# A K/V place inside a shared table tile against a tile of its own, in a hybrid attention and state-space step

## The chip, the core and the metric

The kernel runs on one core of a Trainium2 chip, alone. The metric is the device time of one execution in microseconds. Five engines work side by side, each through its own instruction queue: PE (matmul), DVE, ACT, POOL, and SP, which issues transfers. They meet at semaphores.

## The reference

One layer of a decoder trunk is computed for a prompt of 512 tokens and for one new token of each of 8 sequences. Per token: RMSNorm with modulation, one input projection, then two parallel parts (8 heads of forgetting attention and a diagonal state-space model, S5), one output projection, a gated residual and a final norm.

```python
h = _rmsnorm(x, g_norm) * (1 + scale[:, None]) + shift[:, None]
p = h @ w_in                                    # q, k, v, z_att, fl, u, z_ssm
# prompt: causal attention over 512 tokens; S5 scan over 512 steps
# decode: each of 8 sequences attends to 4096 past rows in 32 pages
k_past = cache_k[l][page_table].reshape(nb_s, -1, ATT_HEADS, HEAD_DIM)
v_past = cache_v[l][page_table].reshape(nb_s, -1, ATT_HEADS, HEAD_DIM)
s_past = einsum('nthd,nphd->nhtp', q, k_past) * scale + suffix + cnew
pr = softmax(concatenate([s_past, s_new]))
o = einsum('nhtp,nphd->nthd', pr, v_past) + pr_new * v_new
...
mix = concatenate([att * silu(z_att), ssm], axis=-1)
return x + gate[:, None] * (mix @ w_out)
```

All of it is float32. The past rows of K and V are 2 x 64 MB, most of what is read.

## The kernel before

**Two streams of work.** `prompt()` makes the prompt's part: the projections, the S5 phase (`ssm_phase`), attention (`attn`), the output projection. `decode()` works through 64 units of K and 64 of V, each a [128 x 2048] tile of 1 MB (8 sequences x 8 chunks of 512 rows). A K unit is one indirect gather issued by POOL (`gather`); POOL multiplies two of its four parts by q and DVE the other two, ACT sums one part and DVE reduces three into the scores `sc`. A V unit is four pages of 256 KB, each issued by SP (`page`: a load of the page number from `prow`, then the transfer); page j fills the partitions j, j+4, j+8 and so on. PE alone reads V units, into the accumulator `pv`. V of a unit follows K ten units behind (`LAG`).

**Where units lie.** `kvt()` hands out five places in turn: units 0 and 1 of every five go into the arena `arA`, the other three into the ring `kva` (tiles named kv). `arA` is one SBUF tile of 128 x 12864 float32 in which an `Arena` cuts out column ranges by hand: first two K/V places of 2048 columns, then m8, m9, pz0, pz1 and others. The later columns hold what S5 works on (X, U, Hst, gr, gi, ta) and pz, the decode weights that PE reads beside V; the columns of the two places hold small tables for S5 (vec, an, cn, bn0, bn1, lam, mag, ...) before the first K unit comes.

**What sets the order.** Nothing runs where it is written. `Plan.add` records each operation with the exact cells that it touches, `Plan.order` plays the recorded work through a table of costs and picks at each step the ready operation with the lowest key (its number, plus `RANK` by part and engine, plus `TURN` by step), and `issue` hands all of it to the engines in that order. The layer below then adds the semaphore waits. It goes by the tiles of the program: where it cannot tell two accesses of one tile apart, it orders them as the plan has them, with a wait. All operations are recorded through one helper, so the profile shows nearly all of them at one line, L560; L770 and L771 are `page`.

In `ssm_phase`, four rounds q work through gr, gi, ta, tb_ on DVE; each ends with four steps that write 64 partitions of Hst:

```python
V.tensor_mul(ta, gr, (wr, wi)[i])
V.tensor_mul(tb_, gi, (wi, wr)[i])
for gh in range(2):
    rows = slice(64 * gh, 64 * gh + 64)
    V.tensor_tensor(Hst[64 * i:64 * i + 64, g0:g0 + 4, 1:], ta[rows], tb_[rows], ...)
```

In the trace these are the DVE steps TENSOR_TENSOR arA<-arA 64x256. The names in the trace: arA and arB are the arenas, kv the ring, mm, tr, q and pv are PSUM tiles, w and qk hold weights, hT the normed prompt, sc scores.

Of the kernel before, what the change touches and what calls it, by code (L numbers as in the profile page):

```python
# [26 lines left out]
NG = 32  # L27
# [7 lines left out]
AK = 50.25  # L35
# [7 lines left out]
    "e": [-9378, -12179, -17159, -20880, -7129, -3740],  # L43
    "k": [104, -5305, 5846, 4790, -7019, -5420],
    "v": [3806, 19560, 20236, 14005, 5324, 4733],
    "a": [8219, -3833, 15753, 8603, -6405, -12004],
    "b": [4421, -21319, -12840, -4994, 6926, 7303],
    "c": [18435, -15510, 7896, -467, -6963, 4257],
    "d": [-1470, -22153, -9218, 15147, -17350, 1823],
# [6 lines left out]
    ],  # L56
    "d": [
        4795, 6712, 1132, 822, -677, -645, 961, 271, -1496170991788475374953747049762376384512,
        -1591416928304185771207288444586741267955712, -15098942732813808483527931238350312571928576,
        -24799897758268515043116245559766386923798528, -24799957837215446326703523194706079082610688,  # L60
        -22512543007516039504454457036779652038787072, -25002668463705283549291374098367526039715840,
        -29873932956061450741600537962173382751420416, -40522577413528868136961928381290713911918592,
        -656491679919118699897556014178701078953984, -642743040628110155344957322818619348877312,
        -62820075513418327778175664689033788658810880, -31965431385341246944872999212492328399798272,
        -32190172543624901591007866841660712573468672, -662031355379155916244683619416854488940544,
        -106016004103496999941151100604199043334144, -662031355379155916244683619416854488940544,
        -661537939003796413634398241935909585944576, -661537939003796413634398241935909585944576,
        -662031355379155916244683619416854488940544, 29, 268848616566157757319417064656553902080,
        -57870939370597673452547150700062179328, -334202152619078557839858215189636710400,
        -222824342116560032991352920573877420032, -525646652941556557807465459025453252608, 423,  # L70
        -3114873590464629931083284636405596160, -383115191651056941544106031232183173120,
        -386230065241521609254121178825750478848, -355144111998878565346486905165379010560,
        -64470733409659124669137878287273426944, -536450766638600210376872646191683207168,
        -442246846342626279238667934105147015168, -550661652511238445432594584645721391104,
        -647779345490100210706929550522845233152, -647779345490100210706929550522845233152,
        -586050504110921321804771991115117101056, -444201669966760682229681522505072771072,
        -377431746165918168997425053696, -372824414621113103280408363008, -372824414621113103280408363008,
        -1504693897653695397102722742222848, -1504693897653695397102722742222848,
        -1935208998083464046905965777610648584192, -9878709610588491638058856337331527352320,
        -21914172760187454673687602720408004984832, -19930248552996642265506833922142981062656,  # L80
        -35472622895141998128347479877853969907712, -17942108367032813781047609379774116397056,
        -21914172760187454673687602720408004984832, -22295873388539040105921799003631698051072,
        13483862984301235780786450122486151380992, 35430370893032923703480572196236596084736,
        -62262870277911108193245080439253630976, -31852081206274918821088721330146711175168,
        -57312208504676145128161655563302161350656, 296716, 799, 1375, 1151, -6151969445025, -890395425558722,
        -156758765851781088, -156758765851781088, -196442193167641696, 6151969415511, -18965520271643, -37818,
        -893, -1054, 20313999, 20314729, 21951, -11686584, -11698753, -9559, -1020863, -496961, 487489, 540935,
        53762, -671, 105, -169, 28310960870464548, -895, -191, -463, 238, 2053, 5138895284143988736,
        5138895284143988736, 1074408661396193280, 2120, 337884334897070912, 337884334897070336,
        337884334897069824, -32645103648539280408576, 838, 833, 863, 2307, -25873837905436944899419790114816,  # L90
        -25873837905436944899419790114816, -25873837905436944899419790114816,
        -52309082650344698289716512553959424, -167332142037711083914639474098700288,
        -182522220296334633003524770624438272, -115023059387366376401550924689965056,
        -167306268199805658525976698141278208, -115023059387366376401550924689965056,
        -313445072502919342502520957467361280, -345069178162099110757908700360343552,
        -1586434662390481495591677170024448, -4400390153836027197102747969126400,
        -6000515168275917989466142700208128, 7115305423999194397066622140416, 0,
        7115305423999201152466063196160, 6755399441065209
    ],
# [69 lines left out]
class Arena:  # L169


    def __init__(self, t, start=0):
        self.t, self.at, self.names = t, start, {}

    def tile(self, shape, dtype, name, bufs=1, room=0):
        n = max(room, int(np.prod(shape[1:])))
        if name not in self.names:
            self.names[name] = [self.at, n, bufs, 0]
            self.at += n * bufs
            assert self.at <= self.t.shape[1], (name, self.at)  # L180
        e = self.names[name]
        assert n <= e[1], name
        o = e[0] + e[1] * (e[3] % e[2])
        v = self.t[:shape[0], o:o + int(np.prod(shape[1:]))]
        e[3] += 1
        if len(shape) > 2:
            ax = "abcd"[:len(shape) - 1]
            v = v.rearrange(f"p ({' '.join(ax)}) -> p {' '.join(ax)}", **dict(zip(ax, shape[1:])))
        return v


class Plan:
# [128 lines left out]
    def cost(self, eng, method, args, outs, ins, kw):  # L321
        n = max([r[4] for r in outs + ins], default=1)
        ps = any(r[5] for r in outs + ins)
        if "dma" in method:
            return (955 if "indirect" in method else 560) if eng == "Pool" else 800 if method == "dma_page" else 480
# [242 lines left out]
def tile_fox_s5_step(ctx, tc, x_prompt, x_sample, c_prompt, c_sample, cache_k, cache_v, cache_logf,  # L568
# [18 lines left out]
    plan.own(arA)  # L587
    plan.own(arB)
# [37 lines left out]
    for at, lst in (("kv", (("vec", 128), ("xs64", 128), ("bad", 128), ("an", 256), ("ldt", 32), ("cn", 512), ("bn0", 1024),  # L626
# [1256 lines left out]
```

## Time and profile before

| what | value |
|---|---|
| median of 3 runs | 615.48 us (613.07 to 615.69) |
| the profiled execution | 620.36 us, its span 618.0 us |
| TensorE clock granted, mean | 0.888 |
| busy PE / DVE / ACT / POOL | 478.5 / 388.5 / 286.9 / 264.5 us |
| moved by DMA | 178.71 MB, mean 289 GB/s |
| DMA queues' share of 16 engines | 50.5% (SP's), 29.1% (POOL's) |

The profiled execution is one run with the profiler on; sums are made against its span of 618.0 us, and it lies 0.8% above the median. Busy time is per engine and overlaps; which wait ends last in a stage tells what that stage costs.

### The profile page before, as it was taken

The page shows a single profiled execution, that of the slowest core. Times are in us where ns is not written, and L with a number is a line of the kernel's source. Part 1 is how long each engine was busy: PE and PEld are TensorE (multiplying, and loading weights), DVE is VectorE, ACT ScalarE, POOL GpSimd, SP SyncE. Part 2 cuts the span into 40 slices and gives each one's busy share as a digit, 9 for nine tenths or more (in the row PEclk, how much of TensorE's full clock was granted, in tenths as well). Part 3 has the DMA queues.
Part 4 walks back from the last instruction along what each step waited for, and adds up shares of the span by engine and source line. Part 5 has one row for each costly group of instructions (what it writes and reads, how often), then busy time and mean ns, then how long its engine had stood idle before and what let it go on. Part 6 is the DMA issues. An engine that isn't in the chain of part 4 may idle for free.

```text
span 618.0 us, 10616 instructions
## 1 busy us (share of the span) xinstructions
PE 478.5 (77%) x3203; PEld 252.1 (41%) x3203; DVE 388.5 (63%) x660; ACT 286.9 (46%) x1369; POOL 264.5 (43%) x201
## 2 busy tenths in 40 slices
PE   2768999779956573835676996979979798999872
PEld 2237347636522252614543442434434453433321
DVE  5999788494467927955764766565573744765321
ACT  2532366442244812424453698566675863432000
POOL 3188399551134843442444445263362344441000
PEclk9969999969986875975897997988999897999975
DMA  7993897664758986695899779899999699998850
GB/s 239 398 356 106 322 288 275 237 229 132 266 190 283 332 336 229 224 373 154 297 343 383 283 290 351 317 398 336 351 391 360 252 358 417 351 348 290 276 205 3
DMA packets 56849, 178.71 MB, mean 289 GB/s; under 512 B 18354, under 2 KB 33112, under 8 KB 39256
## 3 DMA queue, kind: packets, MB, share of 16 engines
q1 hardware_dynamic: 46560, 109.35, 50.5%
q0 software_dynamic: 10016, 68.63, 29.1%
q8 instruction: 25, 0.41, 0.3%
q14 instruction: 32, 0.26, 0.1%
q10 hardware_dynamic: 216, 0.06, 0.0%
HBM read 172.53 MB, written 5.47 MB: 288 GB/s over the span
## 4 chain that ended last, share of the span: by engine, by line
PE 38%; DMA 27%; DVE 12%; SPq 7%; ACT 6%; issue 5%; POOL 2%; POOLq 0%; DVEq 0%; ACTq 0%
PE mm L560 29%; DMA arA<-in_cache_v_dram 8%; DVE arA L560 7%; DMA kv<-in_cache_v_dram 6%; DMA arA<-in_cache_k_dram,kidx 5%; PE pv L560 5%; PE tr L560 4%; DMA kv<-in_cache_k_dram,kidx 4%; SPq L771 4%; SPq L770 2%; ACT arA L560 2%; DVE sc L560 2%; ACT arB L560 2%; DMA w<-in_w_out_dram 1%; DVE arB L560 1%
## 5 line engine op out<-in xcount | busy, mean ns | idle before, releaser
L560 POOL TENSOR_TENSOR kv<-kv,qs 128x1024 f32<-128x1024 f32 x38 | 89.6, 2359 | 79.6 <-DMA kv<-in_cache_k_dram,kidx 61.1
L560 ACT ACTIVATE kv<-kv 128x64 f32<-128x64 f32 x304 | 73.1, 243 | 78.6 <-DVE kv L560 66.7
L560 PE MATMUL mm<-hT,w 128*128 128x512 f32 x224 | 103.3, 617 | 0.0
L560 POOL DMA_INDIRECT kv<-in_cache_k_dram,kidx x38 | 37.9, 997 | 109.5 <-DVE sc L560 18.9
L560 DVE TENSOR_REDUCE sc<-kv 128x24 f32<-128x1536 f32 x38 | 66.3, 1747 | 17.0 <-POOL kv L560 16.8
L560 PE MATMUL mm<-w,hT 128*64 128x256 f32 (+1 forms) x384 | 62.7, 399 | 17.4 <-DVE arA L560 13.3
L560 POOL TENSOR_TENSOR arA<-arA,qs 128x1024 f32<-128x1024 f32 x26 | 61.4, 2364 | 30.9 <-DMA arA<-in_cache_k_dram,kidx 24.0
L560 ACT ACTIVATE arA<-arA 128x64 f32<-128x64 f32 (+2 forms) x219 | 52.8, 245 | 40.1 <-DVE arA L560 37.3
L560 PEld LDWEIGHTS mm<-w,hT 128*64 128x64 f32 (+1 forms) x384 | 53.1, 204 | 28.1 <-DVE arA L560 14.2
L560 PEld LDWEIGHTS mm<-hT,w 128*128 128x128 f32 x224 | 43.5, 199 | 51.2 <-issue 50.7
L560 DVE TENSOR_TENSOR kv<-kv,q 128x1024 f32<-128x1024 f32 x38 | 46.1, 1212 | 26.0 <-DMA kv<-in_cache_k_dram,kidx 25.5
L560 PE MATMUL pv<-kv,arA 128*32 128x512 f32 x304 | 45.5, 679 | 21.6 <-DMA kv<-in_cache_v_dram 21.5
L560 ACT ACTIVATION_READ_ACCUMULATOR kv<-kv 128x1 f32 x304 | 57.2, 188 | 0.0
L560 DVE TENSOR_REDUCE sc<-arA 128x24 f32<-128x1536 f32 x26 | 45.4, 1747 | 13.4 <-POOL arA L560 12.9
L560 DVE TENSOR_TENSOR arA<-arA 128x32 f32<-128x32 f32 (+8 forms) x80 | 31.9, 420 | 27.7 <-DMA arA<-in_cache_v_dram 25.5
L560 ACT ACTIVATION_READ_ACCUMULATOR arA<-arA 128x1 f32 x208 | 39.3, 189 | 0.0
L560 PE MATMUL pv<-arA 128*32 128x512 f32 x208 | 30.3, 663 | 11.0 <-DMA arA<-in_cache_v_dram 11.0
L560 POOL DMA_INDIRECT arA<-in_cache_k_dram,kidx x26 | 25.5, 981 | 23.7 <-PE pv L560 12.9
L560 DVE TENSOR_TENSOR arA<-arA,q 128x1024 f32<-128x1024 f32 x26 | 31.4, 1209 | 5.4 <-DMA arA<-in_cache_k_dram,kidx 5.3
L560 PE MATMUL mm<-w,arB 128*128 128x512 f32 x64 | 31.6, 650 | 2.9 <-DMA w<-in_w_out_dram 2.9
L560 ACT ACT_TABLE_LOAD x23 | 29.5, 1283 | 6.3 <-DVE sc L560 3.3
L560 ACT ACTIVATE arB<-tr 128x512 f32<-128x512 f32 (+3 forms) x46 | 20.8, 479 | 25.0 <-PE tr L560 15.3
(253 smaller groups left out, 765.9 us busy)
## 6 DMA issues: line engine op xcount, KB each, us to landing
kv<-in_cache_v_dram SPq DMA_DIRECT2D x152, 256.0 KB
arA<-in_cache_v_dram SPq DMA_DIRECT2D x104, 256.0 KB
w<-in_w_in_dram SPq DMA_DIRECT2D x11, 1024.0 KB
w<-in_w_ada_dram SPq DMA_DIRECT2D x9, 1024.0 KB
qk<-in_w_ada_dram SPq DMA_DIRECT2D x2, 1024.0 KB
kv<-in_x_prompt_dram SPq DMA_DIRECT2D x2, 1024.0 KB
w<-in_w_out_dram SPq DMA_DIRECT2D x2, 1024.0 KB
qk<-in_w_out_dram SPq DMA_DIRECT2D x2, 1024.0 KB
```

What stands on the lines that cost most here:

```text
L560: fn(*args, **kw)
L770: v = nc.values_load(at, engines=[mybir.EngineType.SP], skip_runtime_bounds_check_because="pages of the pool")
L771: return nc.sync.dma_start(out[0], in_[bass.DynSlice(v, 1)].rearrange("n r x -> (n r) x"))
```

## The change

Two tiles of their own, kv0 and kv1 (named kv_83 and kv_84 in the built program), take the places of the first 4096 columns of arA, which shrinks by as much. The early tables move with them: the small ones into kv0, bn0 and bn1 into kv1. `kvt()` hands out kv1 and kv0 in turn where it handed out the arena's two. The planner's cost of a page on SP goes from 800 to 970 ns. `RANK` and `TURN`, which hold the order, are new throughout. The same operations are recorded as before. The helper's line is now L593, `page` L809 and L810.

```diff
-AK = 50.25
+AK = 34.25
 RANK = {
-    "e": [-9378, -12179, -17159, -20880, -7129, -3740],
+    "e": [-14411, -25244, -19742, -16758, -20859, -859],
...
 class Arena:
     def __init__(self, t, start=0):
-        self.t, self.at, self.names = t, start, {}
+        self.t, self.at, self.names, self.sub = t, start, {}, {}
     def tile(self, shape, dtype, name, bufs=1, room=0):
+        if name in self.sub:
+            return self.sub[name].tile(shape, dtype, name, bufs)
...
-            return (955 if "indirect" in method else 560) if eng == "Pool" else 800 if method == "dma_page" else 480
+            return (955 if "indirect" in method else 560) if eng == "Pool" else 970 if method == "dma_page" else 480
...
-    plan.own(arA)
-    plan.own(arB)
+    places = [ar.tile([128, 2048], F32, name=f"kv{i}") for i in range(2)]
+    for t in (arA, arB, *places):
+        plan.own(t)
...
-    for name, size, bufs in (("kv", 2048, 2), ("m8", NG * (NCH + 1), 1), ("m9", 2304, 1), ("pz0", 1024, 1), ("pz1", 1024, 1),
+    for name, size, bufs in (("m8", NG * (NCH + 1), 1), ("m9", 2304, 1), ("pz0", 1024, 1), ("pz1", 1024, 1),
...
+    for t, lst in ((places[0], (("vec", 128), ("xs64", 128), ("bad", 128), ("an", 256), ("ldt", 32), ("cn", 512), ("tmpc", 128),
+                                ("th", 64), ("nn", 64), ("lam", 64), ("mag", 64), ("sn_t", 128), ("dt", 32), ("lrd", 32),
+                                ("am1", 32), ("t1", 32), ("t2", 32), ("den2", 32))),
+                   (places[1], (("bn0", 1024), ("bn1", 1024)))):
+        a = Arena(t)
+        for name, size in lst:
+            a.tile([128, size], F32, name=name)
+            tb.sub[name] = a
...
-        if kvp[1] is not None and n % 5 in (0, 1):
-            return kvp[1].tile([128, 2048], F32, name="kv", bufs=2)
+        if n % 5 in (0, 1):
+            kvp[1] += 1
+            return places[kvp[1] % 2]
         return kva.tile([128, 2048], F32, name="kv")
```

**SP in the S5 phase.** The four pages of one V unit in arA, before; in brackets are the semaphores each waits for. DMAHW and DMASW are landings of transfers issued by SP and by POOL; each transfer of SP waits for the eighth before it.

```order
L771 DMA arA<-in_cache_v_dram 32x2048 [waits DMASW5_49,DMAHW4_49,DVE_49,Activation_49]
L770 TENSOR_LOAD prow
L771 ISA
L771 DMA arA<-in_cache_v_dram 32x2048 [waits DMAHW5_49,DVE_49]
...
L771 DMA arA<-in_cache_v_dram 32x2048 [waits DMAHW6_49]
...
L771 DMA arA<-in_cache_v_dram 32x2048 [waits DMAHW7_49,DVE_49]
```

The same unit now:

```order
L810 DMA kv_84<-in_cache_v_dram 32x2048 [waits DMASW5_49,DMAHW3_49,DVE_49,Activation_49]
L809 TENSOR_LOAD prow
L810 ISA
L810 DMA kv_84<-in_cache_v_dram 32x2048 [waits DMAHW4_49]
...
L810 DMA kv_84<-in_cache_v_dram 32x2048 [waits DMAHW5_49]
...
L810 DMA kv_84<-in_cache_v_dram 32x2048 [waits DMAHW6_49]
```

The second and the fourth page no longer wait for DVE; the first still waits for the K unit that lay there.

**DVE at the same place,** the third round of S5 with its steps on Hst (64x4x64), before:

```order
L560 TENSOR_TENSOR arB<-mm,arB 64x32 [waits PE_49]
L560 TENSOR_TENSOR arB<-mm,arB 64x32
L560 TENSOR_TENSOR arA<-arA 64x4x64 [waits DMAHW5_49,DMAHW4_49,DMAHW6_49,DMAHW3_49,DVE_49]
L560 TENSOR_TENSOR arA<-arA 64x4x64 [waits DMAHW6_49,DMAHW5_49]
L560 TENSOR_TENSOR arB<-mm,arB 64x32 [waits PE_49]
```

And now:

```order
L593 TENSOR_TENSOR arB<-mm,arB 64x32 [waits PE_49]
L593 TENSOR_TENSOR arB<-mm,arB 64x32
L593 TENSOR_TENSOR arA<-arA 64x4x64 [waits DVE_49]
L593 TENSOR_TENSOR arA<-arA 64x4x64
L593 TENSOR_TENSOR arB<-mm,arB 64x32 [waits PE_49]
```

The steps stand where they stood; their waits for landings of V pages (DMAHW) are gone.

**PE at the end,** from the last scoring (the first product of each fence) on, before; pv rows are V units, mm rows with w or qk and arB are the output projection of the prompt:

```order
L560 MATMUL tr_476<-ident_95,mx_475 8x128
L560 MATMUL pv_346<-kv_474,arA_81 32x512 x4
L560 MATMUL pv_346<-kv_478,arA_81 32x512 x4
...
L560 MATMUL mm_537<-w_503,arB_82 128x512 x4
L560 MATMUL mm_537<-w_502,arB_82 128x512 x4
L560 MATMUL pv_346<-arA_81 32x512 x8
...
L560 MATMUL mm_539<-qk_505,arB_82 128x512 x4
L560 MATMUL mm_539<-qk_504,arB_82 128x512 x4
```

And now:

```order
L593 MATMUL tr_478<-ident_97,mx_477 8x128
L593 MATMUL pv_348<-kv_476,arA_81 32x512 x4
L593 MATMUL pv_348<-kv_480,arA_81 32x512 x4
...
L593 MATMUL mm_531<-qk_507,arB_82 128x512 x4
L593 MATMUL mm_531<-qk_506,arB_82 128x512 x4
...
L593 MATMUL mm_541<-qk_507,arB_82 128x512 x4
L593 MATMUL mm_541<-qk_506,arB_82 128x512 x4
...
L593 MATMUL mm_539<-w_505,arB_82 128x512 x4
L593 MATMUL mm_539<-w_504,arB_82 128x512 x4
```

One more projection group now stands between the last scoring and the last V unit. On SP two of the stores of y now stand directly ahead of the last unit's four pages, where before one stood ahead of an earlier unit.

More of the change, by code (lines that the diff above doesn't have):

```diff
@@ L42 @@
 RANK = {
-    "e": [-9378, -12179, -17159, -20880, -7129, -3740],
[L44 to L49, printed above, removed]
+    "e": [-14411, -25244, -19742, -16758, -20859, -859],
+    "k": [18397, -15550, 8591, 7953, -12240, -6546],
+    "v": [-9085, 12810, 29056, -6364, 8398, -88],
+    "a": [11830, 1247, 22656, -16707, -7001, -6671],
+    "b": [-4277, -15538, -32314, 5089, -4287, 4755],
+    "c": [22088, -2732, 13492, -3209, -10103, 18389],
+    "d": [-8859, -26750, 3767, 21817, 7887, 437],
 }
@@ L52 @@
     "e": [
[3 rows of a table removed]
[3 rows of a table added]
     ],
     "d": [
[L58 to L96, printed above, removed]
@@ L97 @@
-        -6000515168275917989466142700208128, 7115305423999194397066622140416, 0,
-        7115305423999201152466063196160, 6755399441065209
[66 rows of a table added]
     ],
     "p": [
[10 rows of a table removed]
+        -109, 15, 45, -222, 8065, 9977, 1242, 643, 11365, -490, -52652, -6798, -44945, -48680, -1887, 28198,
+        28540, 29652, 29644, 0, -81618134797231127511251775270519595367956360312478778144486273843200, 0,
+        -18373, 0, -5779, 0, 21, 0, 42497621235554144873424195564477612032,
+        42497621235554144873424195564477612032, 42497621235554144873424195564477612032, -565, -7857, 1978, 9191,
@@ new lines @@
+        2407, 29285, 29684, -15877, -1343, -14927, -13852, 10816, 4340329273, 4340489340, 4340480743, -2764,
+        6198, -877, 245, 35416023233, 4473, -422, 7706, 10730, 12618, 144, 11243, 1224, 34937, 8517930800,
+        8517932124, 8517931362, 8517932246, 26435093416, 42435016302974063345664, 42435016302974063345664,
+        42435016302974063345664, 127839947401898655481856, 35353015588, 84869968819851064508416,
+        -1690998123043453585927812582427070562304, 5353620633031020109512982426285980516352,
@@ new lines @@
+        3662912131573146954534552254631685128192, 7044618756074473695440795008713051078656,
+        7044618756074473695440795008713051078656, 7582, 30998918359293790244597937974071315286540810434117632,
+        30998918350070824823780670117331434463764334923218944,
+        30998918441720504955920491051401361979759328965427200, 77417908100936604894132400352864162356920320,
+        -16905104742501867612434523550789078857285632, 8509675778110755114046603593808924454694118303146704896,
+        7786776666398760674500781184652224857538262789739511808,
@@ L111 @@
+        12460596675090748511242188559371858885320015025069359104
     ],
@@ L622, in tile_fox_s5_step @@
     late = Arena(arA)
-    for name, size, bufs in (("kv", 2048, 2), ("m8", NG * (NCH + 1), 1), ("m9", 2304, 1), ("pz0", 1024, 1), ("pz1", 1024, 1),
+    for name, size, bufs in (("m8", NG * (NCH + 1), 1), ("m9", 2304, 1), ("pz0", 1024, 1), ("pz1", 1024, 1),
                              ("y_sv", 512, 1), ("u_s", 512, 1), ("oT", 32, 1)):
         late.tile([128, size], F32, name=name, bufs=bufs)
-    for at, lst in (("kv", (("vec", 128), ("xs64", 128), ("bad", 128), ("an", 256), ("ldt", 32), ("cn", 512), ("bn0", 1024),
[3 rows of a table removed]
+    for t, lst in ((places[0], (("vec", 128), ("xs64", 128), ("bad", 128), ("an", 256), ("ldt", 32), ("cn", 512), ("tmpc", 128),
[6 more added lines that the diff above has]
+            tb.sub[name] = a
+    for at, lst in (("m8", (("cT", 1024), ("tC", 512), ("tB", 512))),
                     ("m9", (("Bsw", 512), ("pw", 576), ("Am", 72), ("Bm", 72), ("Fst", 128), ("fr", 64),
@@ L854, in tile_fox_s5_step @@
     plan.after(W["q", 1])
-    kvp = [0, late]
+    kvp = [0, 0]
     def kvt():
@@ L1424, in attn @@
         attT = res["attT"]
-        spare = Arena(arA, kvp[1].names["gr"][0])
+        spare = Arena(arA, late.names["gr"][0])
         cum = spare.tile([8, S], F32, name="cum")
@@ L1624, in sample_kv @@
             SP.dma_start(xs2[32 * j:32 * j + 8], dap(x_sample, 256 * j, [[D, 8], [1, 256]]))
-    kvp[1] = m8p[0] = m8p[1] = late
+    m8p[0] = m8p[1] = late
     y_sv, u_s = (svec(n, late) for n in ("y_sv", "u_s"))
```

85 rows, old and new, of tables (TURN, late) are left out of this document.

## The prediction

> **What bounds the kernel now.** I read the page first, then the table by stages, the waits, and the chain of work that ended last in the stage with the lowest PE share.
>
> ```profile
> span 618.0 us, 10616 instructions
> ...
> PE 478.5 (77%) x3203; PEld 252.1 (41%) x3203; DVE 388.5 (63%) x660; ACT 286.9 (46%) x1369; POOL 264.5 (43%) x201
> ...
> DMA packets 56849, 178.71 MB, mean 289 GB/s; under 512 B 18354, under 2 KB 33112, under 8 KB 39256
> ...
> PE 38%; DMA 27%; DVE 12%; SPq 7%; ACT 6%; issue 5%; POOL 2%; POOLq 0%; DVEq 0%; ACTq 0%
> PE mm L560 29%; DMA arA<-in_cache_v_dram 8%; DVE arA L560 7%; DMA kv<-in_cache_v_dram 6%; DMA arA<-in_cache_k_dram,kidx 5%; PE pv L560 5%; PE tr L560 4%; DMA kv<-in_cache_k_dram,kidx 4%; SPq L771 4%; SPq L770 2%; ACT arA L560 2%; DVE sc L560 2%; ACT arB L560 2%; DMA w<-in_w_out_dram 1%; DVE arB L560 1%
> ...
> kv<-in_cache_v_dram SPq DMA_DIRECT2D x152, 256.0 KB
> arA<-in_cache_v_dram SPq DMA_DIRECT2D x104, 256.0 KB
> ```
>
> No engine is full. In the chain's last line stands the oddity: landings of V pages in arA hold 8% of the span, more than those in the kv ring (6%), though the ring takes 152 pages and arA 104.
>
> ```profile
> 0.00:100.00 100.00, 75.26 (x514) 40.62 (x516) 84.24 (x223) 41.98 (x169) 61.48 (x64) 0.95 0.83 285
> 100.00:175.00 75.00, 67.25 (x544) 44.48 (x540) 45.35 (x79) 27.00 (x146) 30.29 (x27) 0.93 0.66 235
> 175.00:300.00 125.00, 70.74 (x581) 44.21 (x583) 85.77 (x119) 52.72 (x292) 56.70 (x36) 0.76 0.72 254
> 300.00:575.00 275.00, 239.32 (x1432) 112.89 (x1429) 163.57 (x218) 163.58 (x760) 114.58 (x73) 0.94 0.92 343
> 575.00:600.00 25.00, 19.73 (x97) 6.25 (x95) 7.00 (x17) 1.15 (x2) 0.74 (x2) 0.90 0.79 263
> 600.00:618.00 18.00, 6.21 (x46) 3.66 (x42) 2.56 (x7) 0.51 (x2) 0.74 (x2) 0.50 0.01 2
> ```
>
> Columns: stretch, length, busy PE, PEld, DVE, ACT, POOL, PE clock, DMA share, GB/s. From 300 to 575 us the K/V stream (0.92 of the DMA engines) and PE (87%) share the work. From 175 to 300 us, the S5 phase, nothing is full: PE 57%, DVE 69%, DMA 0.72. There the waits decide:
>
> ```profile
> DVE arA L560 <- DMA arA<-in_cache_v_dram: 37.9, 9, 8.7
> ...
> POOL arA L560 <- DMA arA<-in_cache_v_dram: 6.3, 1, 6.3
> ...
> SPq L771 <- DVE sc L560: 35.4, 8, 8.7
> SPq L771 <- DVE arA L560: 31.3, 6, 7.9
> ```
>
> (The last two are SyncE's own waits, 100 to 300 us.) DVE and POOL never read a V page; only PE does. So 37.9 + 6.3 = 44.2 us are waits for a landing in other columns of the same tile, and SyncE's 31.3 us ahead of a page are mostly the same seen from the other side. The chain shows both sides at once:
>
> ```profile
> 220.11 8.33 DMA arA<-in_cache_v_dram
> ...
> 228.61 0.43 DVE arA L560
> 229.06 0.48 SPq L771
> 229.58 0.27 SPq L770
> 230.03 4.98 DMA arA<-in_cache_v_dram
> 235.10 0.43 DVE arA L560
> 235.55 2.98 DMA arA<-in_cache_v_dram
> 238.62 0.43 DVE arA L560
> ...
> 242.45 9.36 PE mm L560 x32
> ```
>
> A page lands, one 0.43 us DVE step runs, only then does SyncE send the next page, and the next DVE step waits for that. Two queues that share no data hand each other on for 18.5 us (220.1 to 238.6).
>
> **The change part by part.** *The places become tiles.* In the new order no DVE, ACT or POOL step on arA waits for a page, and of a unit's four pages only the first waits for an engine. Instructions, bytes and tile sizes stay. What it is worth is read from the engine that goes on after each episode, not from the sum of the idle time (windows 100:130, 175:200, 215:245, 255:285):
>
> ```profile
> PE tr L560 <- POOL arA L560: 6.0, 1, 6.0
> ...
> DVE arA L560 <- DMA arA<-in_cache_v_dram: 4.1, 1, 4.1
> ...
> DVE arA L560 <- DMA arA<-in_cache_v_dram: 15.5, 3, 8.7
> PE mm L560 <- DVE arA L560: 13.3, 1, 13.3
> ...
> PE tr L560 <- DVE sc L560: 11.5, 1, 11.5
> DVE arA L560 <- DMA arA<-in_cache_v_dram: 10.0, 3, 4.6
> ```
>
> Episode one: DVE and then POOL (its 6.3) waited one after the other, PE only 6.0 for both; PE carries on, so 6.0. Two: 4.1. Three: PE stood 13.3 while DVE stood 15.5; 13.3. Four: 10.0 of PE's 11.5. Sum 33.4 us. The upper end is 44.2. The lower end comes from DVE: 27.4 us out of 125 leave 97.6 us for 85.8 us of DVE, 88%; the fullest stretch above has 84%, at which 85.8 us need 102 and only 23 come out, so 29 in all. I take 33.4, since the first end counts time in which PE had work and the second presumes that DVE's own work cannot be moved into the next stage (59% there). Late next is then the K gather and the reduction of it (the "DVE sc" that SyncE waits for, 35.4 us), a true dependency.
>
> *The clock.* PE runs at 0.76 from 175 to 300 us, where it waits, and at 0.94 from 300. The 9.36 us group behind episode three would be shorter at full clock, by 4.7 at the most and 0 at the least; I take 2. [...]
>
> *The new order at the end.* Between the last scoring and the end stand ten V units as before, but three projection groups instead of two on PE.
>
> ```profile
> 570.78 7.07 PE mm L560 x16
> ...
> 582.88 8.38 SPq L771 DMA_DIRECT2D arA<-in_cache_v_dram  x8
> 591.82 3.37 SPq L771 DMA_DIRECT2D kv<-in_cache_v_dram  x4
> 595.29 0.53 SPq L560 DMA_DIRECT2D out_dram<-hT  x1
> ...
> 594.72 3.36 DMA kv<-in_cache_v_dram
> ```
>
> Here SyncE's issuing, about 1 us a page, is the pace, and PE idles 5.3 of the 25 us. A 7.07 us group moved into these gaps is worth 0 to 5.3; two y stores that now stand ahead of the last four pages cost 0.53 each, and up to one group, 7.07, if their DVE step is late. Between +5 and -8 I take a gain of 3.
>
> *Free edits.* The early tables lie in the two places instead of in arA's first columns; the first two gathers keep their positions on POOL behind the same gate, so nothing; were that cover gone, it would move two gathers by a microsecond or two. The planner's cost of a page (970 for 800) runs on no engine; the timeline's 8.38 us for eight pages says it is nearer the truth. The state stores and x_sample loads moved between pages on SyncE: about 0.5 us of issue each, hidden while the stream has pages in flight.
>
> Sum: 33.4 + 2 + 3 = 38.4; 618.0 - 38.4 = 579.6 us of span. The profiled run took 620.36 us, 2.4 beside its span, and lies 4.9 above the median of 615.48; so 579.6 + 2.4 - 4.9 = **577 us**.
>
> **The rivals.** *The stream sets the pace earlier (faster still).* DMA work is 0.83 x 100 + 0.66 x 75 + 0.72 x 125 + 0.92 x 275 + 0.79 x 25 = 495 us; if the 412 us behind the first 100 run at 0.92, that is 448, and with 100 in front and 18 behind a span of 566: **564 us**. For it speaks that the ping-pong held back SyncE too, against it that DVE would have to reach 90%.
>
> *DVE and POOL collide (smaller gain).* From 175 to 300 us:
>
> ```profile
> L560 DVE TENSOR_TENSOR arA<-arA 128x256 f32<-128x256 f32 x6 | 8.5, 1416 | 0.0
> L560 DVE TENSOR_TENSOR arA<-arA,arB 128x256 f32<-128x256 f32 x12 | 7.1, 614 | 0.1
> L560 DVE TENSOR_TENSOR arA<-arA 64x256 f32<-64x256 f32 x12 | 5.0, 414 | 25.6 <-DMA arA<-in_cache_v_dram 25.5
> ```
>
> The first two do the same amount of work and differ by 0.8 us each; I take a collision with POOL's products as the cause. POOL is busy 45% there and would be 58% of 97.6 us. If the twelve also go to 1416 ns, 9.6 us are lost, and with DVE's ceiling the gain is 29 - 9.6 = 19: **596 us**. [...]
>
> *No change.* The waits removed only hide true waits for K: SyncE's 35.4 us on DVE sc might grow by what DVE no longer waits. Against it: DVE's idle time in S5 stands almost whole in the one row of 64x256 steps above (25.5 of 25.6), not in rows that wait for gathers. **615 us**.
>
> *Slower.* The new order lets the second half run dry. By 300 us the stream had moved 28.5 + 17.6 + 31.8 = 78 MB; if S5 ends 33 us earlier with the same 78 MB, 101 MB of the 178.7 remain, which at 343 GB/s take 294 us (span about 267 + 294 + 18 = 579, my forecast again). It turns slower below 101 MB / 333 us = 303 GB/s, for which SyncE would have to wait some 40 us more in that half; at 290 GB/s the span is 633: **631 us**.
>
> **How the numbers follow.** The forecast's own case (568 to 588) 0.55; stream-paced 0.2; collision 0.15; no change 0.04; slower 0.06. The likeliest gives 577. From 558, a little under the stream-paced 564, to 598, a little over the collision's 596, little more than 1 in 10 is left out. Half a per cent, 3 us, is about what this kernel's runs can tell from no change: faster 0.91, same 0.03, slower 0.06.
>
> **What would show it.** Right: no "DVE arA <- DMA" of a V page in the waits, SyncE's "<- DVE arA" under 5 us, DVE above 80% and the DMA share above 0.8 in the S5 phase, and PE's clock there near 0.9. The end term is right if PE idles under 4 us in the last 25 us before the last page lands. Wrong: 128x256 steps on arA at 1.4 us throughout (collision), GB/s under 303 in the second half (slower), or waits for gathers in DVE's list where the page waits stood (no change).

## The result, and the profile after

| kernel | time, us | runs | profiled span, us | TensorE clock |
|---|---|---|---|---|
| before | 615.59 median (613.07 to 617.59) | 4 | 618.0 | 0.888 |
| changed | 586.34 median (584.08 to 590.48) | 4 | 584.4 | 0.907 |

The ratio is 0.9535, with a 95% interval of 0.9471 to 0.9598: faster by some 29 us. The forecast was 577. Medians here are of all runs, while ratios and intervals leave out runs that lie more than 1.5% above the fastest of the same kernel.

The page of the changed kernel, its first lines, the DMA total, and the chain of work that ended last by engine and by line:

```profile
span 584.4 us, 10616 instructions
...
PE 473.4 (81%) x3203; PEld 246.1 (42%) x3203; DVE 390.0 (67%) x660; ACT 293.5 (50%) x1374; POOL 267.7 (46%) x201
...
DMA packets 56849, 178.71 MB, mean 306 GB/s; under 512 B 18354, under 2 KB 33112, under 8 KB 39256
...
PE 30%; DMA 19%; DVE 18%; issue 11%; POOL 9%; SPq 6%; ACT 5%; POOLq 0%; DVEq 0%; ACTq 0%
PE mm L593 22%; DMA kv<-in_cache_k_dram,kidx 9%; DMA kv<-in_cache_v_dram 8%; POOL kv L593 7%; PE pv L593 6%; DVE arA L593 5%; DVE sc L593 4%; DVE arB L593 3%; SPq L810 3%; DVE kv L593 3%; PE tr L593 3%; ACT kv L593 2%; SPq L809 2%; DMA kv<-in_b_im_dram 1%; DMA w<-in_w_in_dram 1%
```

The work is the same to within 7 us on every engine; the span is 33.6 us shorter. The landings of V pages in arA (8% of the chain) are gone, and K landings lead the DMA part.

The changed kernel by stages (busy PE, PEld, DVE, ACT, POOL, then PE clock, DMA share, GB/s):

```profile
100.00:175.00 75.00, 67.66 (x571) 44.06 (x567) 53.11 (x92) 34.86 (x181) 34.76 (x29) 0.98 0.72 251
175.00:300.00 125.00, 96.74 (x782) 57.60 (x786) 97.84 (x138) 64.28 (x329) 62.88 (x40) 0.88 0.91 336
300.00:550.00 250.00, 212.32 (x1209) 92.58 (x1202) 143.23 (x190) 151.32 (x691) 104.40 (x65) 0.90 0.90 337
```

From 175 to 300 us PE does 96.7 us of work where it did 70.7, and the stream moves 336 GB/s where it moved 254. From 300 us on little is different in kind.

What the engines wait for now, whole span, engine's waits and then SyncE's:

```profile
POOL kv L593 <- DMA kv<-in_cache_k_dram,kidx: 103.3, 32, 8.3
...
DVE kv L593 <- DMA kv<-in_cache_k_dram,kidx: 47.2, 18, 7.8
...
SPq L810 <- DVE sc L593: 62.4, 17, 8.9
...
SPq L810 <- PE pv L593: 30.6, 8, 8.7
SPq L810 <- DMA kv<-in_cache_k_dram,kidx: 21.6, 4, 6.5
```

No wait of DVE or POOL on arA for a V page is left, and no wait of a page for DVE on arA. POOL and DVE wait for K units to land, and a page waits for the K unit in its place to be scored or for PE to have read the V unit there. These are true dependencies.

Where the time stands along the span (start of the instruction in the profiled execution, us):

| | before | changed | old order, tiles | changed, half V bytes |
|---|---|---|---|---|
| last 64x256 step of S5 | 280.9 | 232.8 | 246.2 | 235.1 |
| 9th of 32 row maxima of attention | 377.4 | 331.0 | 344.8 | 331.2 |
| 25th | 466.7 | 438.9 | 436.5 | 427.7 |
| 4th of 8 scorings of K (DVE, mx) | 314.5 | 285.1 | 280.4 | 284.9 |
| 8th | 564.7 | 530.1 | 532.6 | 516.2 |
| last V product | 599.0 | 567.0 | 566.9 | 552.8 |
| span | 618.0 | 584.4 | 585.5 | 571.1 |

The changed kernel is 48.1 us ahead at the end of S5, 46.4 at the ninth maximum, 27.9 at the 25th, and 33.6 at the end. These first three marks belong to the prompt. The K units were never 48 us ahead: their fourth scoring is 29.4 us earlier, their eighth 34.6. A part of the 48 is only that the new order takes S5 earlier among the other work: on the old tile (the first experiment) it ends S5 9.9 us ahead of the kernel before and finishes 17.0 behind. The last two columns belong to experiments below.

### The profile page after: what moved, and what is told of

Read it like the earlier page. It is cut to its first block, busy times and chain, and to the rows that moved or that the text cites. A ratio compares the mean times of both kernels' runs of the same rounds, so it can differ in the third digit from the quotient of the medians.

```text
span 584.4 us, 10616 instructions
## 1 busy us (share of the span) xinstructions
PE 473.4 (81%) x3203; PEld 246.1 (42%) x3203; DVE 390.0 (67%) x660; ACT 293.5 (50%) x1374; POOL 267.7 (46%) x201
## 3 DMA queue, kind: packets, MB, share of 16 engines
q0 software_dynamic: 10016, 68.63, 30.7%
## 4 chain that ended last, share of the span: by engine, by line
PE 30%; DMA 19%; DVE 18%; issue 11%; POOL 9%; SPq 6%; ACT 5%; POOLq 0%; DVEq 0%; ACTq 0%
PE mm L593 22%; DMA kv<-in_cache_k_dram,kidx 9%; DMA kv<-in_cache_v_dram 8%; POOL kv L593 7%; PE pv L593 6%; DVE arA L593 5%; DVE sc L593 4%; DVE arB L593 3%; SPq L810 3%; DVE kv L593 3%; PE tr L593 3%; ACT kv L593 2%; SPq L809 2%; DMA kv<-in_b_im_dram 1%; DMA w<-in_w_in_dram 1%
## 5 line engine op out<-in xcount | busy, mean ns | idle before, releaser
L593 POOL TENSOR_TENSOR kv<-kv,qs 128x1024 f32<-128x1024 f32 x64 | 151.3, 2369 | 124.0 <-DMA kv<-in_cache_k_dram,kidx 103.0
L593 ACT ACTIVATE kv<-kv 128x64 f32<-128x64 f32 (+1 forms) x517 | 124.1, 243 | 123.4 <-DVE kv L593 110.7
L593 DVE TENSOR_REDUCE sc<-kv 128x24 f32<-128x1536 f32 x64 | 111.5, 1745 | 34.1 <-POOL kv L593 33.9
L593 DVE TENSOR_TENSOR kv<-kv,q 128x1024 f32<-128x1024 f32 x64 | 77.4, 1213 | 59.7 <-DMA kv<-in_cache_k_dram,kidx 47.2
L593 POOL DMA_INDIRECT kv<-in_cache_k_dram,kidx x64 | 63.9, 998 | 106.2 <-PE pv L593 30.7
L593 PE MATMUL mm<-hT,w 128*128 128x512 f32 x224 | 104.6, 622 | 0.1
L593 ACT ACTIVATION_READ_ACCUMULATOR kv<-kv 128x1 f32 x512 | 96.1, 188 | 0.0
L593 PE MATMUL pv<-kv,arA 128*32 128x512 f32 x512 | 73.1, 678 | 24.6 <-DMA kv<-in_cache_v_dram 20.6
L593 PEld LDWEIGHTS mm<-hT,w 128*128 128x128 f32 x224 | 43.7, 200 | 53.2 <-issue 51.6
L593 PE MATMUL mm<-w,hT 128*64 128x256 f32 (+1 forms) x384 | 60.4, 392 | 3.5 <-ACT e L593 3.5
L593 PEld LDWEIGHTS mm<-w,hT 128*64 128x64 f32 (+1 forms) x384 | 51.7, 200 | 14.3 <-ACT e L593 5.2
L593 ACT ACT_TABLE_LOAD x28 | 35.9, 1283 | 13.7 <-DVE sc L593 10.3
L593 PEld LDWEIGHTS pv<-kv,arA 128*32 128x32 f32 x512 | 13.7, 115 | 62.9 <-issue 53.2
L593 PE MATMUL mm<-qk,arB 128*128 128x512 f32 x64 | 31.3, 646 | 5.2 <-DVE e L593 4.6
L593 ACT ACTIVATE arB<-tr 128x512 f32<-128x512 f32 (+3 forms) x46 | 21.0, 474 | 15.3 <-PE tr L593 15.1
L593 PE MATMUL mm<-w,arB 128*128 128x512 f32 x64 | 28.5, 598 | 0.2 <-DMA w<-in_w_out_dram 0.2
L593 DVE TENSOR_TENSOR arA<-arA 64x256 f32<-64x256 f32 (+8 forms) x54 | 27.3, 511 | 1.0 <-ACT arA L593 0.5
L593 DVE TENSOR_TENSOR e<-mm,arB 128x512 f32<-128x512 f32 (+1 forms) x10 | 6.3, 633 | 23.8 <-PE mm L593 23.8
L593 PEld LDWEIGHTS mm<-qk,arB 128*128 128x128 f32 x64 | 12.9, 207 | 21.3 <-issue 15.1
L593 PE MATMUL mm<-w,hTs 128*32 128x64 f32 (+2 forms) x576 | 17.3, 248 | 4.9 <-ACT qk L593 3.0
L593 DVE TENSOR_TENSOR arB<-arB,arA 128x512 f32<-128x512 f32 (+5 forms) x28 | 18.5, 681 | 2.8 <-ACT arB L593 2.8
L593 ACT ACTIVATE arB<-mm,nm 128x128 f32<-128x128 f32 (+3 forms) x32 | 16.7, 524 | 6.6 <-DVE nm L593 6.5
```

Source lines behind the costliest of these rows:

```text
L593: fn(*args, **kw)
```

## The experiments

Each was timed against the kernel before on the same chip; spans and rows are those of the profiled executions.

**Tiles and order apart.** The first two runs cross the change's two halves.

```diff
-    places = [ar.tile([128, 2048], F32, name=f"kv{i}") for i in range(2)]
+    places = [arA[:, 2048 * i:2048 * i + 2048] for i in range(2)]
```

> The changed kernel with the two places put back as columns 0 to 4095 of arA; its order of instructions is the new one on all five engines, row for row, so only the waits inside the shared tile return (32 of DVE, 8 of ACT and 7 of POOL for a V page that shares no cell with them). Theory 'waits' (the removed waits are the gain): 605 to 620 us, with 30 us or more of DVE and POOL waits for V pages in the S5 phase again. Rival 'order' (the new order earns it): 584 to 594 us, the same waits present but covered by other work.

Measured: 636.21 us, ratio 1.0296 (1.0228 to 1.0364). In its profile the waits are back, and SyncE's ahead of its pages with them:

```profile
DVE arA L593 <- DMA arA<-in_cache_v_dram: 42.5, 8, 8.5
...
SPq L810 <- DVE arA L593: 26.5, 6, 8.7
```

"Waits" expected 605 to 620 and "order" less; it came out above both. The new order by itself does not gain, it loses some 18 us on the old tile. Only the tiles stand between this run and the changed kernel, and its span is 50.6 us longer (635.0 against 584.4).

The second run is the kernel before with the places and the early tables as the diff of the change has them, and RANK, TURN and the cost of 800 left as they were.

> The kernel before with nothing changed but the places: tiles of their own, early tables in them; its order of instructions is the old one on all five engines, row for row. Theory 'waits': 584 to 596 us. Rival 'order': 606 to 617 us, since the old order was laid out around the waits and what DVE no longer waits for pages it waits for K.

Measured: 587.67 us, ratio 0.9516 (0.9453 to 0.9579), no different from the changed kernel's 0.9535. Its stages:

```profile
175.00:300.00 125.00, 91.21 (x764) 56.82 (x757) 97.03 (x137) 59.40 (x327) 66.82 (x43) 0.81 0.92 337
300.00:550.00 250.00, 226.42 (x1251) 100.49 (x1252) 150.15 (x198) 148.49 (x685) 99.61 (x64) 0.94 0.91 338
```

With not one instruction in another place, the span is 32.5 us shorter. The tiles alone carry the whole gain: 32.5 us in the old order, 50.6 in the new. In the old order S5 is 34.7 us ahead and 32.5 are still there at the end.

**One place at a time.** The old order with tiles, but one place a column range of arA:

```diff
-    places = [ar.tile([128, 2048], F32, name=f"kv{i}") for i in range(2)]
+    kv = ar.tile([128, 2048], F32, name="kv1")
+    places = [arA[:, 0:2048], kv]
```

> The old order with only one of the two places as a tile of its own (the one with bn0 and bn1); the other stays in arA. Of DVE's 39 false waits for V pages 20 remain, of POOL's 7 and ACT's 8 four each. Theory 'waits add up': about half of the 32.5 us comes, 598 to 607 us. Rival 'one is enough to hand the queues on': 609 to 618 us, since each unit in the shared place stops DVE and SyncE as before. Rival 'slack': 586 to 594 us, the waits that remain lie in time that other work covers.

> The mirror of the run with one place: the place with the small tables is a tile of its own, the other stays in arA; 20 of DVE's false waits remain here too, and PE's four. If the waits add up, the two mirrors together miss about what both places give: this one 598 to 607 us and the sum of the two gains 25 to 40 us. 609 to 618 us if one shared place is enough to stop the queues.

Measured: 597.74 us, ratio 0.9638 (0.9560 to 0.9717), and for the mirror 599.99 us, 0.9731 (0.9671 to 0.9791); the first 0.3 below its range, the second inside. The gains are 3.6% and 2.7% against 4.8% for both places, by the medians 18.6 and 16.3 us against 30.7: about half each, and together somewhat more than both, by less than the runs of the first kernel scatter (588.4 to 604.2 us). The last 64x256 step of S5 shows it more closely: it starts 18.1 and 17.7 us earlier, 35.8 together, against 34.7 with both.

**Why the layer below could not tell the columns apart.** The old order and the shared tile, with the rows of a page in neighbouring partitions:

```diff
-        return nc.sync.dma_start(out[0], in_[bass.DynSlice(v, 1)].rearrange("n r x -> (n r) x"))
+        return nc.sync.dma_start(out[1], in_[bass.DynSlice(v, 1)].rearrange("n r x -> (n r) x"))
...
-  [kv_t[n][j:128:4]]
+  [kv_t[n][j:128:4], kv_t[n][32 * j:32 * j + 32]]
```

> The kernel before, shared tile and old order unchanged, but page j of a V unit is written to the 32 partitions from 32j on, in place of j, j+4, j+8 and so on; bytes, transfers and instructions are the same (V rows then meet the scores of other rows, so y_s differs). No wait of DVE, ACT, POOL or PE on a V page of other columns is left in the built program; 25 waits of SyncE's transfers on each other and 7 of POOL's gathers on each other inside arA stay. If the stride over partitions is why the layer below cannot tell the columns apart: 584 to 598 us, like the old order with tiles. If the shared tile costs by itself (its remaining waits between transfers): 605 to 617 us.

Measured: 702.96 us, ratio 1.132 (1.1218 to 1.1421): far outside both ranges. What DVE and POOL wait for V pages in arA fell from 37.9 and 6.3 us to this:

```profile
DVE arA L560 <- DMA arA<-in_cache_v_dram: 4.1, 1, 4.1
...
POOL arA L560 <- DMA arA<-in_cache_v_dram: 2.4, 1, 2.4
```

So the stride over partitions is what made most of these waits; the columns are the same. S5's last step came 4.1 us earlier all the same. The time is lost elsewhere, in the stream:

```profile
300.00:550.00 250.00, 181.46 (x1142) 89.84 (x1140) 117.07 (x157) 128.23 (x591) 86.43 (x52) 0.81 1.00 260
```

The DMA engines are busy all the time and move 260 GB/s, against 346 at a share of 0.92 in the kernel before. The next run puts the same write pattern on the changed kernel:

> The changed kernel (places of their own) with page j of a V unit written to the 32 partitions from 32j on (y_s differs, as in the old order). There are no waits left for this to remove, so it measures the write pattern by itself: with it the old order took 703 us, DMA share 1.00 at 260 GB/s from 300 to 550 us against 0.92 at 346. Theory 'pattern' (transfers into 32 neighbouring partitions are slower): 670 to 710 us, DMA share 0.98 or more, under 275 GB/s. Rival 'shared tile' (the loss comes from the transfers' waits on each other in arA): 584 to 600 us.

Measured: 715.95 us, beside 616.54 for before, slightly above the range of "pattern"; the DMA share and rate are as it said:

```profile
285.00:500.00 215.00, 148.82 (x850) 68.07 (x850) 104.33 (x134) 111.35 (x502) 75.74 (x46) 0.79 1.02 262
```

So it is the pattern and not the shared tile. The queues' table gives its price. Before:

```profile
q1 hardware_dynamic: 46560, 109.35, 50.5%
q0 software_dynamic: 10016, 68.63, 29.1%
```

and with neighbouring partitions in the old order:

```profile
q1 hardware_dynamic: 46560, 109.35, 60.2%
q0 software_dynamic: 10016, 68.63, 31.7%
```

50.5% of 618.0 us is 312 us of 16 engines for SyncE's 109 MB, 60.2% of 703.7 us is 424, 36% more for the same bytes; POOL's gathers, which were not touched, went from 180 to 223 us. V pages are 67 of the 109 MB, and they carry the loss: from 300 to 550 us a packet of 8 KB on SyncE's queue took 350 ns on average before and takes 570 so. What makes a packet into neighbouring partitions take longer was not tried by itself. The way to be rid of the waits is the tile, not the pattern.

**What sets the pace after S5.** The changed kernel with half of each V page; the products read the first half twice.

```diff
-        return nc.sync.dma_start(out[0], in_[bass.DynSlice(v, 1)].rearrange("n r x -> (n r) x"))
+        return nc.sync.dma_start(out[0][:, 0:1024], in_[bass.DynSlice(v, 1)].rearrange("n r x -> (n r) x")[:, 0:1024])
```

> The changed kernel with each V page cut to its first 1024 columns (128 KB in place of 256 KB) and the V products reading those columns twice; 33.6 MB of 178.7 are not moved, the number of transfers, pages on SyncE and matmuls stay, and so does the order. It asks what sets the pace after the S5 phase, where the 48 us won there shrank to 33. Theory 'stream' (the bytes set the pace from 285 us on): 33.6 MB at 337 GB/s are 100 us of stream, of which PE's own work (212 of the 250 us from 300 on) leaves at most 38 to win: 545 to 565 us. Rival 'PE' (its work sets the pace and the DMA share of 0.90 only runs along): 580 to 587 us. Rival 'places' (units wait for K landings and the reduction, not for bandwidth): 568 to 580 us.

Measured: 570.83 us, ratio 0.9224 (0.9155 to 0.9294), 13.3 us of span below the changed kernel, all of it behind the ninth maximum of attention (331.2 us against 331.0; table above). That lies in the range of "places" and outside "stream" and "PE". The range alone does not decide for "places", since with fewer V bytes the K units land sooner too (POOL waits 68.9 us for them in place of 103.3). What is shown is that the bytes hold back 13 us there and that another limit stands close behind. The changed kernel, and with half the V bytes, in the same stretch:

```profile
285.00:500.00 215.00, 182.44 (x1082) 80.52 (x1080) 126.88 (x165) 147.81 (x658) 94.87 (x57) 0.90 0.92 348
```

```profile
285.00:500.00 215.00, 185.49 (x1132) 82.70 (x1131) 137.26 (x171) 149.79 (x674) 98.78 (x60) 0.93 0.82 296
```

The same cut in the old order with tiles:

> The old order with both places as tiles and V pages of 128 KB, each V product reading the first 1024 columns twice. In the new order the same cut gave 571 us, 15 less, all of it behind 331 us, where the 46 us won by then were otherwise given back. In the old order S5 won only 34.7 us, and they were kept to the end. Theory 'the stream's pace is 584 to 588 us in either order': the cut gives about as much here, 568 to 577 us. Rival 'in the old order the prompt sets the end': 580 to 588 us.

Measured: 558.78 us, ratio 0.9046 (0.8992 to 0.9100), lower than either expected: 25.0 us of span less than with whole pages. With whole pages both orders run at one pace, 348 and 347 GB/s at 0.92 from 285 to 500 us, and end 1.1 us apart; with half of the V bytes they end 10.6 apart, the old order first. Its row:

```profile
285.00:500.00 215.00, 197.23 (x1167) 90.83 (x1168) 135.12 (x175) 146.59 (x673) 101.00 (x63) 0.93 0.82 297
```

This fits a stream that holds both orders and makes them tie. Once it is lighter, the old order has less in its way, not more.

Is the other limit PE? V products of 256 columns in place of 512, but for the first and last of each accumulation:

```diff
+    def pvmm(out, lhsT, rhs, **k):
+        n = 512 if k["start"] or k["stop"] else 256
+        plan.add("PE", "matmul", lambda o, l, r, **kw: nc.tensor.matmul(o[:, :n], l, r[:, :n], **kw), (out, lhsT, rhs), k)
```

> The changed kernel with 408 or more of the 512 V products cut from 512 to 256 columns of V (the other columns of y_s are left out); bytes, transfers, order and all other work stay. The V products took 73.1 us of PE (512 at 678 ns), so some 30 us of PE's 473 go. With half the V bytes the time fell to 571 us, 15 less, and PE was busy 88% of 300 to 550 us there. Theory 'PE' (PE's work is the pace after the S5 phase, and the bytes are a second limit close behind): 562 to 574 us. Theory 'stream': 581 to 588 us. Rival 'places' (a V unit's place comes free sooner when PE reads it in less time): a few us, 576 to 583.

> Both cuts together: V pages of 128 KB and V products of 256 columns. If stream and PE are two limits that take turns, cutting both gives more than the sum of each alone: 535 to 555 us. If what is left is the K units (gather, products, reduction through five places), which neither cut touches: 562 to 571 us, about as with half the bytes alone.

Measured: 595.26 us, ratio 0.9667 (0.9560 to 0.9775), no gain, and above every range; with both cuts 572.25 us, 0.9280 (0.9244 to 0.9315), about as with the bytes alone. PE's work in V products went down from 73.1 to 44.0 us, and with half the bytes from 66.6 to 42.4. But all of PE's busy time fell only from 473.4 to 457.4 us and from 466.9 to 458.1, and the granted clock fell too: 0.907 to 0.891, and 0.922 (half the bytes) to 0.882 (both). The V products' rows with both cuts, and the granted clock of that kernel:

```profile
L648 PE MATMUL pv<-kv,arA 128*32 128x256 f32 x480 | 37.6, 423 | 13.0 <-DMA kv<-in_cache_v_dram 13.0
...
L648 PE MATMUL pv<-kv,arA 128*32 128x512 f32 x32 | 4.8, 680 | 2.0 <-issue 2.0
```

```profile
core 0: 572.0 us, clock 0.882
```

Less V work alone brings no time. Whether PE as a whole is the limit can't be said from it, since about half of what was taken away came back as longer work elsewhere on PE. Both cuts together came out 1.3 us above the range named for K units (562 to 571).

POOL's product of each K unit cut to half:

```diff
-                e.tensor_tensor(kr[:, lo:hi], kr[:, lo:hi], q[:, None, :].to_broadcast([128, hi - lo, 512]), op=OP.mult)
+   for POOL: nc.gpsimd.tensor_tensor(o[:, :, 0:256], x[:, :, 0:256], y[:, :, 0:256], op=OP.mult)
```

> The changed kernel with POOL's product of each K unit cut from 1024 to 512 columns (the scores are then wrong in that part); order, bytes and the other engines' instructions stay. 64 products of 2369 ns become about 1.2 us each: some 75 of POOL's 268 us go, and with them half the time in which POOL can hold up DVE's two-input steps. Theory 'collision' or 'POOL' (they set the pace of K units): 560 to 575 us, the 128x256 and 64x256 steps of S5 near 420 ns. Rival 'stream and PE': 580 to 588 us, POOL's waits for K landings longer by about what its work is shorter.

Measured: 588.85 us, ratio 0.9538 (0.9473 to 0.9602), the changed kernel's own. (The profiled execution, 597.73 us, is the longest of its four runs, its span 11.4 us over the changed kernel's.) POOL's row:

```profile
L1540 POOL TENSOR_TENSOR kv<-kv,qs 128x512 f32<-128x512 f32 x64 | 81.7, 1280 | 155.6 <-DMA kv<-in_cache_k_dram,kidx 125.3 <-ACT qs L593 21.2 <-DMA kv<-in_cache_v_dram 8.6
```

70 us less of POOL's work, and POOL waits 125.3 us for K landings where it waited 103.3, of which the longer span may be up to half. Its product is not the pace.

**Another order.** The changed kernel's tables, planned with the old cost:

```diff
-... 970 if method == "dma_page" else 480
+... 800 if method == "dma_page" else 480
```

> The changed kernel with the planner's cost of a page put back from 970 to 800 ns: tiles and the tables RANK and TURN as changed, and the order that comes out differs on all engines from about 200 us on. The cost runs on no engine; what is measured is what another order of the same work is worth once the false waits are gone. Theory 'the order earns nothing by itself': 583 to 595 us. Rival 'the order is fitted to 970': 600 to 620 us.

Measured: 624.19 us, ratio 1.0105 (1.0036 to 1.0173): 38 us over the changed kernel (30 between the profiled spans, 614.3 and 584.4), all of the gain lost with the tiles in place. It lies above the rival's range too. The K units keep up (the fourth scoring starts at 282 us, in the changed kernel at 285), S5 ends 3.9 us earlier, and then the ninth maximum of attention starts at 366.3 us in place of 331.0. The changed kernel, and this one, in that stretch:

```profile
330.00:366.00 36.00, 31.75 (x128) 13.69 (x126) 23.99 (x32) 24.41 (x116) 17.77 (x11) 0.86 0.89 340
```

```profile
330.00:366.00 36.00, 18.87 (x72) 5.36 (x72) 22.11 (x24) 15.65 (x96) 18.04 (x12) 0.55 0.94 353
```

PE is busy 18.9 of 36 us at a clock of 0.55 while the stream is full. Its waits there:

```profile
PE pv L593 <- DMA kv<-in_cache_v_dram: 10.4, 3, 4.0
PE tr L593 <- DVE mx L593: 5.8, 1, 5.8
```

The prompt's products stand in PE's queue behind V products that wait for their pages and behind a scoring (tr<-mx) that waits for its row maxima. An order can cost tens of us; that the old and the new one tie is a property of these two.

## Why the prediction was right, and where it was off

**The waits (forecast 33.4 us).** Right in mechanism and size. Alone, in the old order, they were worth 32.5 us of span and 34.7 at the end of S5; by single places 18.1 and 17.7. In that run PE carries out the same instructions in the same order, so the traces can be laid side by side: it is 1.0 us ahead of the kernel before in front of episode one, 9.6 behind it, 13.7 behind the second, 25.8 behind the third and its group, 34.7 behind the fourth. The episodes brought 8.6, 4.1, 12.1 and 8.9 us; forecast, with the clock term in the third, were 6.0, 4.1, 15.3 and 10.0. Of the signs named, the page waits went and the DMA share (0.91) and the clock (0.88) came; DVE reached 78% from 175 to 300 us, not 80. Counting each episode by the engine that goes on after it, PE, came nearer than the sum of DVE's and POOL's idle time (44.2) or DVE's ceiling (29). The forecast took the waits and the new order as two terms to be added. The runs show that they are not: the same tiles are worth 50.6 us in the new order, and the new order costs 17.0 us of span without them.

**The clock (forecast 2).** The group that was named did come out so. Before, and in the old order with tiles:

```profile
242.45 9.36 PE L560 MATMUL mm<-w,hT 128*128 128x256 f32 x32 [13.29 <-DVE arA L560]
```

```profile
218.84 7.17 PE L562 MATMUL mm<-w,hT 128*128 128x256 f32 x32 [0.83 <-DVE arA L562]
```

It is 2.2 us shorter, and the wait in front of it is nearly gone. In the trace of before the granted clock is 0.50 from 233.3 to 246.9 us, and a product of the group starts every 0.43 us; behind that it is 1.00, and one starts every 0.21 us. The 4.7 at the most would need 0.50 throughout, where the mean over the group was 0.76. The 2 was the author's choice between the two ends, and no run shows it apart from the waits; what the runs show is the 2.2 us of this group. Waits and clock were 35.4 us together; 34.7 stood at the end of S5 and 32.5 at the end. So most of what is missing was lost behind S5, not in these terms. PE's busy time as a whole did not fall (478.5 to 480.2 us in that run), though the clock from 175 to 300 us rose from 0.76 to 0.81, and to 0.88 in the changed kernel.

**The new order at the end (forecast 3).** Wrong. The sign that was named did come, PE idles 0.1 us of the last 25 before the last page lands, but it did not mean a gain. The kernel before and the changed one, from the last scoring to the end:

```profile
564.75:618.00 53.25, 36.18 (x177) 14.13 (x175) 14.29 (x36) 3.42 (x9) 2.24 (x6) 0.78 0.52 174
```

```profile
530.12:584.40 54.28, 41.84 (x197) 16.97 (x196) 19.26 (x43) 5.85 (x12) 4.32 (x8) 0.88 0.59 195
```

The stretch holds 5.7 us more of PE's work and is 1.0 us longer. The like for like is the old order with tiles:

```profile
532.60:585.50 52.90, 36.31 (x177) 14.45 (x175) 14.30 (x36) 3.42 (x9) 2.25 (x6) 0.78 0.52 171
```

Against it the last scoring comes 2.5 us earlier and the stretch behind it is 1.4 us longer. The group filled the idle time there; why the 7 us that it left free further ahead brought only 2.5 is not shown, and the stream's pace, which both orders share, is a likely reason. The whole new order is worth 1.1 us between the two profiled spans, which these runs cannot tell from nothing.

**From span to median (forecast -2.5).** The forecast carried over that the profiled execution of before lay 4.9 us above its median. That of the changed kernel lies 0.2 below its own, so the median is 1.9 above the span and not 2.5 below it. This is 4.4 of the 9.3 us by which the forecast was low; 2.9 come from the waits and the clock, 1.9 from the order (4.8 of span). An offset of one execution is scatter and says nothing about another kernel.

**The free edits.** The cost of a page runs on no engine, as said, yet it is not free: with 800 ns under the new tables 30 to 38 us go. Tables and cost are one fit, and the step looked only at each edit's own work.

**The rivals.** "The stream sets the pace earlier" was half right. It holds back both orders, but at 585 us and not 566: from 100 to 175 us the share stayed at 0.72 and not 0.92. With half of each V page to move, the new order ends another 13.3 us earlier and the old one with tiles 25.0. "No change" did not come: DVE's waits for K landings grew only from 30.8 us to 34.3 in the old order and 47.2 in the new, and SyncE's for "DVE sc" fell from 73.4 to 62.4. "Collision" did not come in net: from 175 to 300 us the three kinds of steps took 20.6 us before and take 19.3 now, spread otherwise:

```profile
L593 DVE TENSOR_TENSOR arA<-arA 64x256 f32<-64x256 f32 x12 | 8.5, 708 | 0.2
...
L593 DVE TENSOR_TENSOR arA<-arA,arB 128x256 f32<-128x256 f32 x12 | 5.6, 489 | 0.1
L593 DVE TENSOR_TENSOR arA<-arA 128x256 f32<-128x256 f32 x6 | 5.2, 864 | 0.0
```

That POOL is what stretches such steps was shown: with its product cut to half the 64x256 steps of the whole kernel took 447 ns in place of 636, and DVE 377.5 us in place of 390.0. The changed kernel's trace shows it step by step. Of the sixteen 64x256 steps, the two during which a product of POOL runs take 1.9 and 2.4 us, the others at most 0.42. DVE's products of K, which read q from PSUM, take 1.21 us with POOL beside them and without. The time did not move in the run with half of the product, so these steps do not set it. "Slower" needed under 303 GB/s in the second half; it had 337. What was named as late next, the K gathers and their reduction, is: POOL waits 103.3 us for K landings, and SyncE 62.4 us for "DVE sc".

**Open:** what holds the new order at 571 us once the stream is lighter, 10.6 us behind the old order. Less V work on PE did not move it, nor, with whole pages, less of POOL's product. What the traces of the two orders with half pages show is that SyncE and POOL wait 32.0 and 25.0 us for V products of PE in the new order, 11.4 and 16.4 in the old: places come free later. No run tried whether that is the limit. No complete version beat the two that tie.

## What to carry to other kernels

Give every region that a DMA writes a tile of its own when its access steps over partitions: inside a shared tile the semaphores may order it against columns that it never touches (here 44.2 us of DVE's and POOL's waits, and 6.5 without the step), and a wait of an engine for a landing that it does not read is the sign. Count such a wait by the engine that goes on afterwards, then ask what the next limit is; here it was the K/V stream, and half of the V bytes would have brought 13 to 25 us more. And an order made by a planner can depend on the waits and costs that it was made for: the new order lost 18 us without the tiles and 30 to 38 under the old cost, while the old order took the tiles without loss.

## What the runs showed of the hardware

With pages of 256 KB written into 32 neighbouring partitions, and not into every fourth of 128, SyncE's queue took 36% more time of the DMA engines for the same bytes, and the gathers beside it 24% more: 260 GB/s at a share of 1.00 against 346 at 0.92 in the old order, and 262 at 1.02 against 348 at 0.92 in the new. And with half the columns in the V products the granted clock was lower, 0.882 against 0.922 with half the V bytes and 0.891 against 0.907 with all of them. In the first pair, of 24 us less in V products (66.6 to 42.4) only 8.8 us less of PE's busy time were left, and the time did not fall (570.83 and 572.25 us).
